# A row gradient on one core: the first store of each group of three behind most of the second tile's vector pass, that pass in two parts, and more row ends placed by Pool

## The chip, the core and the metric

The kernel runs on one core of a Trainium2 chip, launched once. The core has a vector engine (DVE in the profile), a general engine (POOL, "Pool" here), a queue engine that only issues transfers here (SP, its queue SPq), and 16 DMA engines that move data between the device memory (HBM) and the on-chip memory. A tensor engine and a scalar engine exist and do nothing in this kernel. The metric is the device time of one execution in microseconds; lower is better.

## The reference

```python
def setup_inputs():
    return {
        "x": np.random.randn(8192, 8192).astype(np.float32),
    }

def reference(x: np.ndarray) -> np.ndarray:
    return np.gradient(x, axis=1)
```

Along each row, an inner element of the result is half the difference of its right and left neighbour. The first is x[1] - x[0], the last x[8191] - x[8190], both without the half. 268.44 MB are read and as many written, with one subtraction and one scaling for each element.

## The kernel before

**Tiles.** The 8192 rows are cut into 32 tiles ("sets") of 256 rows: 128 partitions with R = 2 rows each, which lie one behind the other in a partition, W = 16384 float32 columns. There are NB = 3 buffers (`slots`) of SH + W columns with SH = 64. A load writes a tile to columns 64 to 64 + W of its buffer; the result is computed in place, shifted to columns 0 to W, and stored from there. Tile i lives in buffer i % 3.

**Work on a tile**, in the order of the program:

1. Pool takes the differences at the row ends (L70): for both rows of a partition x[1] - x[0] and x[m-1] - x[m-2], into a small tensor `ends` that keeps all tiles' values. It waits for the load.
2. The vector engine makes one pass over the tile (L76), a custom instruction that subtracts and scales by 0.5, columns 1 to W - 1. It waits for Pool's differences, since it writes over the input. At the row ends it leaves wrong values.
3. The row ends are placed over them (L87), four values in a partition, by Pool where i % 5 is 1 or 3 and i < 30, otherwise by the vector engine.
4. SP issues the store (L89), which waits for the placement.
5. After every third tile SP issues the next three loads (L60). Each waits until the store of the tile that had its buffer has landed.

**Order.** The order in each engine's queue is the order of the program (`manual_schedule`). The helper `chain` declares which earlier steps an instruction must wait for, and nothing else is waited for. All 64 transfers go through SP's one queue, in the order three loads, three stores, three loads, and so on; the last group has two tiles. A group is three tiles i with i % 3 = 0, 1, 2: "first", "second" and "third" tile, load and store below. An instruction that waits on SP holds up all that stands behind it there. The first tile's pass and placement run while the second load is transferred, the second tile's while the third load is, the third tile's while the first store is.

Of the kernel before, what the change touches and what calls it, by code (L numbers as in the profile page):

```python
# [1 line left out]

# [4 lines left out]


@with_exitstack
def kernel(  # L10
    ctx: ExitStack,
    tc: tile.TileContext,
    x: bass.AP,
    out: bass.AP,
):

    nc = tc.nc
    P = nc.NUM_PARTITIONS
    n, m = x.shape
    R = 2
    NB = 3  # L30
    SH = 64
    W = R * m
    nsets = n // (P * R)
    f32 = x.dtype

    x_sets = x.rearrange("(s p t) m -> s p (t m)", p=P, t=R)
    out_sets = out.rearrange("(s p t) m -> s p (t m)", p=P, t=R)

    pool = ctx.enter_context(tc.tile_pool(name="pool", bufs=1))
    slots = [pool.tile([P, SH + W], f32, name=f"slot{k}", tag=f"slot{k}") for k in range(NB)]  # L40
    ends = pool.tile([P, nsets, R, 2], f32, name="ends", tag="ends")
    loads, stores = [], [None] * nsets
    in_front = {}

    def chain(i, ins, *needed):

        group, engine = f"slot{i % NB}", ins.ins.engine
        keep = [o.ins for o in needed]  # L50
        if in_front.get(engine, (None,))[0] == group:
            keep.append(in_front[engine][1])
        tc.declare_no_dep(ins.ins, group=group, keep=keep, reason="implied by the needed step")
        tc.add_to_no_dep_group(group, ins.ins)
        in_front[engine] = group, ins.ins
        return ins

    def load(i):
        b = slots[i % NB]
        ins = nc.sync.dma_start(out=b[:, SH : SH + W], in_=x_sets[i])  # L60
        loads.append(chain(i, ins, *([stores[i - NB]] if i >= NB else [])))

    with tc.manual_schedule():
        for i in range(NB):
            load(i)
        for i in range(nsets):
            b = slots[i % NB]
            xin = b[:, SH : SH + W].rearrange("p (t m) -> p t m", m=m)

            ins = nc.gpsimd.tensor_sub(  # L70
                out=ends[:, i, :, :],
                in0=xin[:, :, 1 : m : m - 2],
                in1=xin[:, :, 0 : m - 1 : m - 2],
            )
            at = [chain(i, ins, loads[i])]
            ins = nc.vector._custom_dve(  # L76
                dve_ops.TENSOR_TENSOR_REDUCE_SUB_MAX,
                out=b[:, 1 : W - 1],
                in0=b[:, SH + 2 : SH + W],
                in1=b[:, SH : SH + W - 2],  # L80
                s0=0.0,
                s1=0.5,
            )
            halved = chain(i, ins, *at)
            res = b[:, 0:W].rearrange("p (t m) -> p t m", m=m)
            placer = nc.gpsimd if i % 5 in (1, 3) and i < nsets - 2 else nc.vector
            ins = placer.tensor_copy(out=res[:, :, 0 : m : m - 1], in_=ends[:, i, :, :])  # L87
            placed = chain(i, ins, halved)
            ins = nc.sync.dma_start(out=out_sets[i], in_=b[:, 0:W])  # L89
            stores[i] = chain(i, ins, placed)  # L90
            if i % NB == NB - 1:
                for k in range(i + 1, min(i + 1 + NB, nsets)):
                    load(k)


# [1 line left out]
_INS = ['x']  # L97
_OUTS = [((8192, 8192), 'float32')]


# [23 lines left out]
```

## Time and profile before

| | |
|---|---|
| time, median of 3 runs | 1247.99 us (1247.7 to 1248.6) |
| profiled execution, its own time | 1247.59 us |
| span of its instructions | 1245.7 us |
| moved | 268.44 MB read, 268.44 MB written, 431 GB/s over the span |
| vector engine busy | 554.6 us, 52 instructions |
| Pool busy | 8.8 us, 48 instructions |
| placement L87 on the vector engine | 20 times, mean 172 ns |
| placement L87 on Pool | 12 times, mean 190 ns |
| load, issue to landing, median | 58.0 us |
| store, issue to landing, min / median / max | 20.9 / 40.4 / 41.4 us |

A row of the timeline gives the start and the length in us, the engine, the line, the operation, what it writes and reads, and in brackets how long its engine had been idle and what ended that. Rows of SPq are the issues of transfers; "x3" joins three issues in a row, and the length is then the time from the first to the last. A row of the table by windows gives the window, its length, the busy time of DVE and of POOL with their instructions, the granted clock of the tensor engine (unused here), the share of the DMA engines and GB/s. A packet is put down to the window in which it starts, so in short windows the share can be over 1 or 0 although the engines work throughout. A group row of the page has the line, engine, operation, output and input shape, the number of instructions, busy us, mean ns, and the idle time ahead of them with what ended it.

### The profile page before, as it was taken

The page shows a single profiled execution, that of the slowest core. Times are in us where ns is not written, and L with a number is a line of the kernel's source. Part 1 is how long each engine was busy: PE and PEld are TensorE (multiplying, and loading weights), DVE is VectorE, ACT ScalarE, POOL GpSimd, SP SyncE. Part 2 cuts the span into 40 slices and gives each one's busy share as a digit, 9 for nine tenths or more (in the row PEclk, how much of TensorE's full clock was granted, in tenths as well). Part 3 has the DMA queues.
Part 4 walks back from the last instruction along what each step waited for, and adds up shares of the span by engine and source line. Part 5 has one row for each costly group of instructions (what it writes and reads, how often), then busy time and mean ns, then how long its engine had stood idle before and what let it go on. Part 6 is the DMA issues. An engine that isn't in the chain of part 4 may idle for free.

```text
span 1245.7 us, 237 instructions
## 1 busy us (share of the span) xinstructions
DVE 554.6 (45%) x52; POOL 8.8 (1%) x48
## 2 busy tenths in 40 slices
DVE  2850583069009702850582079009603840591083
POOL 0000000000000000000000000000000000000000
DMA  9999999999999999999999999999999999999999
GB/s 404 438 436 423 427 431 438 438 438 436 436 427 431 425 438 436 425 434 436 429 434 436 434 436 434 436 434 438 419 436 436 434 438 438 431 434 429 429 410 404
DMA packets 9217, 536.88 MB, mean 431 GB/s; under 512 B 1024, under 2 KB 1024, under 8 KB 1024
## 3 DMA queue, kind: packets, MB, share of 16 engines
q1 hardware_dynamic: 9216, 536.88, 99.8%
q14 instruction: 1, 0.01, 0.0%
HBM read 268.44 MB, written 268.44 MB: 431 GB/s over the span
## 4 chain that ended last, share of the span: by engine, by line
another core or an unknown queue 74%; DVE 18%; DMA 3%; issue 2%; POOL 1%; SPq 0%; POOLq 0%
DVE slot L76 18%; DMA slot<-in_x_dram 3%; POOL ends L70 0%; POOL slot L87 0%; SPq L60 0%; POOLq L119 0%; DVE slot L87 0%
## 5 line engine op out<-in xcount | busy, mean ns | idle before, releaser
L76 DVE CUSTOM_DVE_ANT_0 slot<-slot 128x16382 f32<-128x16382 f32 x32 | 551.2, 17224 | 668.7 <-POOL ends L70 668.7
L70 POOL TENSOR_TENSOR ends<-slot 128x4 f32<-128x4 f32 x32 | 6.3, 198 | 989.6 <-DMA slot<-in_x_dram 989.6
L87 POOL COPY slot<-ends 128x4 f32<-128x4 f32 x12 | 2.3, 190 | 207.9 <-DVE slot L76 207.9
L87 DVE COPY slot<-ends 128x4 f32<-128x4 f32 x20 | 3.4, 172 | 0.7
L108 POOL MEMSET const-bfloat16-1.0<- 128x1 bf16 x1 | 0.1, 101 | 0.0
L108 POOL MEMSET const-uint8-127<- 128x1 uint8 x1 | 0.1, 101 | 0.0
L108 POOL MEMSET const-float32-0.0<- 128x1 f32 x1 | 0.1, 98 | 0.2 <-issue 0.2
L108 POOL MEMSET const-float32-1.0<- 128x1 f32 x1 | 0.1, 98 | 0.0
## 6 DMA issues: line engine op xcount, KB each, us to landing
slot<-in_x_dram SPq DMA_DIRECT2D x32, 58.0
out_dram<-slot SPq DMA_DIRECT2D x32, 40.4
```

The costliest lines, as they stand in the source:

```text
L70: ins = nc.gpsimd.tensor_sub(out=ends[:, i, :, :], in0=xin[:, :, 1 : m : m - 2], in1=xin[:, :, 0 : m - 1 : m - 2],)
L76: ins = nc.vector._custom_dve(dve_ops.TENSOR_TENSOR_REDUCE_SUB_MAX, out=b[:, 1 : W - 1], in0=b[:, SH + 2 : SH + W], in1=b[:, SH : SH + W - 2],
L87: ins = placer.tensor_copy(out=res[:, :, 0 : m : m - 1], in_=ends[:, i, :, :])
L108: nc = _bacc.Bacc("TRN2", target_bir_lowering=False, num_devices=1)
```

## The change

Four edits.

- `opens` holds for the second tile of the ten full groups (i % 3 = 1 and i < 30). For it the vector pass goes in two instructions, columns 1 to W - 1 - 1472 and from there to W - 1. The other tiles' passes stay whole.
- The store of the first tile of a group is no longer issued in the first tile's own turn. It stands in SP's queue behind the first part of the second tile's pass in the program, and waits for that part as well as for its own placement (`store_behind`). It is still ahead of the second tile's store.
- Pool places the row ends of the first and third tile of each full group (20 tiles), the vector engine those of the second tile and of the last two tiles (12).
- The stores of the last two tiles, and all second and third stores, are issued in their own turn as before.

```diff
+    LATE = 1472
...
+    def store(i, placed):
+        ins = nc.sync.dma_start(out=out_sets[i], in_=slots[i % NB][:, 0:W])
+        stores[i] = chain(i, ins, placed)
+        return ins
+
+    def store_behind(i, placed, other):
+        tc.add_manual_dep(
+            store(i, placed).ins,
+            other.ins.name,
+            mybir.DependencyInfo(mybir.DependencyClass.Sync, mybir.DependencyReason.DATA),
+            reason="the first store of a group goes behind the second tile's difference",
+        )
...
+            opens = i % NB == 1 and i < nsets - 2
...
-            at = [chain(i, ins, loads[i])]
-            ins = nc.vector._custom_dve(
-                dve_ops.TENSOR_TENSOR_REDUCE_SUB_MAX,
-                out=b[:, 1 : W - 1],
-                in0=b[:, SH + 2 : SH + W],
-                in1=b[:, SH : SH + W - 2],
-                s0=0.0,
-                s1=0.5,
-            )
-            halved = chain(i, ins, *at)
+            halved = chain(i, ins, loads[i])
+            edges = [1, W - 1 - LATE, W - 1] if opens else [1, W - 1]
+            for c0, c1 in zip(edges, edges[1:]):
+                ins = nc.vector._custom_dve(
+                    dve_ops.TENSOR_TENSOR_REDUCE_SUB_MAX,
+                    out=b[:, c0:c1],
+                    in0=b[:, SH + c0 + 1 : SH + c1 + 1],
+                    in1=b[:, SH + c0 - 1 : SH + c1 - 1],
+                    s0=0.0,
+                    s1=0.5,
+                )
+                halved = chain(i, ins, halved)
+                if opens and c0 == 1:
+                    store_behind(i - 1, placed, halved)
             res = b[:, 0:W].rearrange("p (t m) -> p t m", m=m)
-            placer = nc.gpsimd if i % 5 in (1, 3) and i < nsets - 2 else nc.vector
+            placer = nc.gpsimd if i % NB != 1 and i < nsets - 2 else nc.vector
             ins = placer.tensor_copy(out=res[:, :, 0 : m : m - 1], in_=ends[:, i, :, :])
             placed = chain(i, ins, halved)
-            ins = nc.sync.dma_start(out=out_sets[i], in_=b[:, 0:W])
-            stores[i] = chain(i, ins, placed)
+            if i % NB or i >= nsets - 2:
+                store(i, placed)
```

More of the change, by code (lines that the diff above doesn't have):

```diff
@@ L4 @@
 import concourse.tile as tile
-from concourse import bass_utils, dve_ops
+from concourse import bass_utils, dve_ops, mybir
 from concourse._compat import with_exitstack
```

## The prediction

> **What bounds the kernel.** I read the page first: the two engines, the DMA row, the byte counts.
>
> ```profile
> DVE 554.6 (45%) x52; POOL 8.8 (1%) x48
> ...
> DMA  9999999999999999999999999999999999999999
> ...
> DMA packets 9217, 536.88 MB, mean 431 GB/s; under 512 B 1024, under 2 KB 1024, under 8 KB 1024
> ...
> q1 hardware_dynamic: 9216, 536.88, 99.8%
> ...
> L76 DVE CUSTOM_DVE_ANT_0 slot<-slot 128x16382 f32<-128x16382 f32 x32 | 551.2, 17224 | 668.7 <-POOL ends L70 668.7
> ```
>
> The DMA engines are busy in every slice and at 99.8% in sum, the vector engine at 45%, so only the rate of the transfers can change the time. There are 64 transfers (32 loads, 32 stores) of 536.88/64 = 8.39 MB. Of 9216 packets 1024 are tiny, one per engine and transfer (64 x 16); the other 8192 carry 65.5 KB each, 8 per engine and transfer.
>
> Next, the timeline gives the pace. Pool's end differences at L70 start as soon as their load has landed (idle ended by the DMA), so their starts are landing times. Four groups and the last pair, with the queue's first stores:
>
> ```profile
> 40.40 40.06 SPq L89 DMA_DIRECT2D out_dram<-slot  x3
> 42.04 0.20 POOL L70 TENSOR_TENSOR ends<-slot 128x4 f32<-128x4 f32 x1 [19.13 <-DMA slot<-in_x_dram]
> ...
> 62.44 0.20 POOL L70 TENSOR_TENSOR ends<-slot 128x4 f32<-128x4 f32 x1 [2.69 <-DMA slot<-in_x_dram]
> ...
> 157.63 39.09 SPq L89 DMA_DIRECT2D out_dram<-slot  x3
> 159.25 0.20 POOL L70 TENSOR_TENSOR ends<-slot 128x4 f32<-128x4 f32 x1 [1.65 <-DMA slot<-in_x_dram]
> ...
> 178.70 0.20 POOL L70 TENSOR_TENSOR ends<-slot 128x4 f32<-128x4 f32 x1 [19.25 <-DMA slot<-in_x_dram]
> ...
> 974.22 0.20 POOL L70 TENSOR_TENSOR ends<-slot 128x4 f32<-128x4 f32 x1 [19.15 <-DMA slot<-in_x_dram]
> ...
> 993.55 0.20 POOL L70 TENSOR_TENSOR ends<-slot 128x4 f32<-128x4 f32 x1 [19.13 <-DMA slot<-in_x_dram]
> ...
> 1186.93 0.20 POOL L70 TENSOR_TENSOR ends<-slot 128x4 f32<-128x4 f32 x1 [77.07 <-DMA slot<-in_x_dram]
> ...
> 1204.62 19.69 SPq L89 DMA_DIRECT2D out_dram<-slot  x2
> 1206.28 0.20 POOL L70 TENSOR_TENSOR ends<-slot 128x4 f32<-128x4 f32 x1 [19.14 <-DMA slot<-in_x_dram]
> ```
>
> From the first load of a group to its second, the ten full groups take 19.33, 19.36, 19.33, 19.35, 19.33, 19.35, 19.34, 19.34, 19.34 and 19.35, together 193.42, mean 19.34 us. This is the undisturbed transfer, 2.42 us a packet on each engine. From the second to the third they take 20.40, 19.45, 19.51, 20.05, 19.85, 19.79, 19.45, 19.84, 19.33 and 19.36, together 197.03: an **excess of 3.61 us**, and only in the load that has a store behind it. From the third load to the next group's first (three stores and a load) the ten stretches add to 773.77 against 40 x 19.342 = 773.68: nothing to gain there. The rest, 22.71 to the first landing, 19.35 for the last pair and 39.4 after it, has no group's first store in it. So 3.61 us, 0.29% of the time, is all that a change to that store can win by these rows.
>
> Two facts bear on why the third load is late. In the last pair the store was issued at 1204.62, 1.66 us ahead of the landing at 1206.28, and the load took 19.35: no excess. In the ten groups the first store is queued some 21 us ahead (178.70 - 157.63 = 21.07). And the windows of the DMA show how far the engines are in step (a packet counts where it starts):
>
> ```profile
> 58.00:59.00 1.00, 1.00 (x1) 0.00 (x0) 1.00 3.28 983
> 59.00:61.00 2.00, 0.50 (x1) 0.19 (x1) 1.00 0.00 0
> 61.00:62.00 1.00, 0.00 (x0) 0.00 (x0) 1.00 2.28 983
> ...
> 987.00:988.00 1.00, 1.00 (x1) 0.00 (x0) 1.00 0.76 328
> 988.00:989.00 1.00, 1.00 (x1) 0.00 (x0) 1.00 1.36 590
> ```
>
> In the first group 15 of 16 engines (983 GB/s for 1 us = 983 KB, at 65.5 KB each) begin the third load's last packet within one microsecond, start nothing for two, and begin the next packet in 61 to 62: some 3 us for a packet of 2.42. The excess is in that last packet, at the turn from load to store. In the ninth group starts are scattered over all windows, and there is no excess.
>
> **The change, part by part.**
>
> *The later store.* Today SP issues the first store when the first tile's pass and placement end. Afterwards it also waits for the first part of the second tile's pass. That part has 16382 - 1472 = 14910 columns; at 17.224 us for 16382 that is 15.68 us, the second part 1.55 us. From the second load's landing: 0.23 us to the pass (42.04 to 42.27), 15.68, and 0.03 us to the queue (the first placement ends at 40.37, the issue is at 40.40): issue at +15.94. The third load lands at +19.34, so the store is queued 3.40 us ahead instead of 21.07. Its own start-up is not exposed: a store on an idle queue takes 20.9 us at least from issue to landing, thus 20.9 - 19.34 = 1.56 us over its transfer, and 3.40 - 1.56 = 1.84 us of margin remain. Issued at 1204.62, the last pair's store started no packet before 1205.4, then all 16 by 1206.0: 0.8 us from the issue, so the new store reaches the engines about 2.6 us before the landing, when each begins its last packet of the load.
>
> What it is worth I bound from both sides. The last pair's row (lead 1.66 us) prices the excess at nothing: minus 3.61. The groups' rows (21.07) keep it whole: 0. The first group's row, in step and with 1.06 us of excess, would cost ten times 1.06 - 3.61 = plus 7.0. A lead of 3.40 stands nearest to 1.66, so I take **minus 3.61**.
>
> A rule of the Trainium skill speaks against the change: "DMA: Bandwidth & Descriptors", section "Rules for kernel authors", says to issue a DMA early, so that its fixed cost overlaps. By that rule the delay can win nothing, and the sum would be zero or worse; this trace has the early store followed by the slower load, and the late one in the last pair by none. The same page, "Anatomy of one DMA", puts the fixed cost of a transfer near 2.0 us; by it the margin would be 3.40 - 2.0 = 1.4 us, an estimate, where the row of 20.9 leaves 1.84.
>
> *What waits behind the store on SP.* Its own queue holds the second store, the third, then the three loads. The second store follows 1.9 us later (the rest of the pass 1.55, the placement 0.17, hand-offs), 18 us before the first store can have been carried out, so its place in the DMA queue is never empty. The third store and the loads keep their triggers. Cost 0; if the margin of 1.84 us were missed, every microsecond more would be an idle DMA microsecond, ten times over.
>
> *The pass in two parts.* Ten more vector instructions. The smallest vector row, the placement, has 0.172 us, the gap between two dependent ones is 0.03; so 10 x 0.2 us at most, and below nothing isn't possible as the same columns are computed. Cover: the pass ends near +17.5, its placement at +17.9, and the third load lands at +19.34, so 1.4 us of idle vector time takes it. Cost 0, without cover 2 us.
>
> *More placements on Pool.* Now 12 on Pool, afterwards the first and third tile of ten groups, 20; on the vector engine 12 instead of 20. Pool takes 0.190 against 0.172 us, and the hand-off from the pass to the issue 0.29 instead of 0.23 us (157.34 to 157.63; 40.17 to 40.40). The first tile's issue no longer hangs on it, the second tile's moves to the vector engine, and the third store waits behind two stores of 19.3 us. Pool's next end difference comes 1.6 us after the first tile's placement, or 58 us after the third's. Cost 0; without cover 20 x 0.06 = 1.2 us.
>
> **Sum.** 1247.59 (profiled execution's own time; its span is 1245.7, the other 1.9 us lie around it) - 3.61 = 1243.98. The median of the runs is 1247.99, 0.40 over that execution: **1244.4 us**, -0.29%.
>
> **Rivals.**
>
> *The store still arrives too early* (no effect). It reaches the engines while the last packets of the load are under way, and a turn that overlaps reads and writes may need nothing more. For: 2.6 us is a full packet, and in the last pair the queue was already empty (no packet start from 1204.6 to 1205.4). Against: queued 21 us ahead, the store goes with 0.45 us or more of excess in five groups of ten, queued 1.66 us ahead with 0.01, and 3.40 is nearer to the latter. Time 1248.0. Between the two, half of the excess goes: 1246.2.
>
> *Re-alignment* (slower). Engines that have run ahead drain and then all start with the store, as the sixteen did within 1205.4 to 1206.0. The 3 us by which the engines drift apart over the run seem to hide the turn: 1.06 us of excess in step, 0.01 in the ninth group. If the late store puts the engines in step ten times and does not remove the turn, each group pays up to the first one's price: 1248.0 + 7.0 = 1255.0. It decides from an average of 0.36 + 0.25 = 0.61 us of excess a group (2.5 us more in ten). For: the two windows above. Against: the second and third group, hardly apart yet, pay 0.11 and 0.17; and only engines more than about 2 us ahead would wait.
>
> **How the numbers follow.** About 0.2%, 2.5 us, is what a measurement of this kernel tells from no change. Forecast 0.50 (1244.4, own range 1243.2 to 1245.6: the runs' spread of 0.9 us and the 0.1 us of the other stretches below, 1.2 us of lost cover above); half of the excess 0.12 (1246.2); no effect 0.15 (1248.0); re-alignment 0.23 (1250.5 to 1255). Faster: the forecast and a third of the half case, 0.54. Same: the rest of these and no effect, 0.23. Slower: 0.23. The range goes from 1243.2 to 1251.0: it leaves out most of the re-alignment, some 0.19.
>
> **What would show it.** Right: the ten intervals from second to third load add to 193.4 to 194 instead of 197.03, with the first store's issue some 3.4 us ahead of the third landing, and the other stretches unchanged. No effect: still near 197. Re-alignment: all ten nearer to 20.4, and 15 or 16 packet starts within one microsecond at every turn, late groups too. I am wrong altogether if the stretch of three stores and a load grows over 77.4 us, which would mean a queue run dry or a price of the turn moved into the store.

## The result, and the profile after

The changed kernel takes 1250.12 us (median of 22 runs, 1245.17 to 1251.73) where the kernel before takes 1247.88 us in the same comparison (22 runs, 1247.16 to 1249.39). The ratio of the means is 1.0014 with a 95% interval of [1.0008, 1.0021]: slower by 0.14% (0.18% by the medians), a loss clear of noise and smaller than the 0.2% at which the prediction drew its line. The profiled execution took 1249.7 us by its own time, with a span of 1247.6 us against 1245.7.

The page of the changed kernel, its DMA and its passes:

```profile
DMA  9999999999999999999999999999999999999999
...
DMA packets 9217, 536.88 MB, mean 430 GB/s; under 512 B 1024, under 2 KB 1024, under 8 KB 1024
...
q1 hardware_dynamic: 9216, 536.88, 99.8%
...
L106 POOL COPY slot<-ends 128x4 f32<-128x4 f32 x20 | 3.8, 192 | 346.4 <-DVE slot L93 346.4
L106 DVE COPY slot<-ends 128x4 f32<-128x4 f32 x12 | 2.1, 172 | 0.4
```

The DMA engines are as busy as before. No queue ran dry; the same bytes took longer on engines that were always at work. The groups by line with shapes kept apart price the two parts of the pass:

```profile
L93 DVE CUSTOM_DVE_ANT_0 slot<-slot 128x14910 f32<-128x14910 f32 x10 | 156.9, 15691 | 21.2 <-POOL ends L85 21.2
L93 DVE CUSTOM_DVE_ANT_0 slot<-slot 128x1472 f32<-128x1472 f32 x10 | 16.9, 1693 | 0.3
```

Together 17.38 us instead of 17.22, all of it in idle time of the vector engine. The timeline of the first and of the eighth group shows the store where the change puts it:

```profile
42.11 0.20 POOL L85 TENSOR_TENSOR ends<-slot 128x4 f32<-128x4 f32 x1 [1.61 <-DMA slot<-in_x_dram]
...
58.06 21.58 SPq L65 DMA_DIRECT2D out_dram<-slot  x3
...
61.57 0.20 POOL L85 TENSOR_TENSOR ends<-slot 128x4 f32<-128x4 f32 x1 [19.26 <-DMA slot<-in_x_dram]
...
857.50 0.20 POOL L85 TENSOR_TENSOR ends<-slot 128x4 f32<-128x4 f32 x1 [1.65 <-DMA slot<-in_x_dram]
...
873.45 22.44 SPq L65 DMA_DIRECT2D out_dram<-slot  x3
...
877.82 0.20 POOL L85 TENSOR_TENSOR ends<-slot 128x4 f32<-128x4 f32 x1 [20.12 <-DMA slot<-in_x_dram]
```

The first store of the first group is issued at 58.06, 3.51 us ahead of the third landing at 61.57. There the third load takes 19.46 us instead of 20.40: the excess is nearly gone. In the eighth group it takes 877.82 - 857.50 = 20.32, more than the 19.84 of before. In both groups the store is issued 15.95 us behind the second landing, as forecast (15.94); what differs is the third landing. Over the ten groups the third loads take 19.46, 19.50, 19.51, 20.01, 19.35, 20.04, 19.75, 20.32, 19.66 and 20.40, together 198.00 against 197.03 before. The stretches of three stores and a load add to 774.26 against 773.77. With 0.97 and 0.49, and 0.07 in the second loads, 0.08 ahead of the first landing and 0.30 behind the last one, the whole difference of the spans, 1.9 us, is accounted for.

Where the eighth group's 20.32 comes from is seen in the windows around its turn from load to store. A row gives the window, its length, DVE and POOL busy, the clock, the DMA share and GB/s; GB/s times length over 65.5 KB is the number of packets that start, and share times length times 16 over that number is the mean time of one of them:

```profile
872.20:872.80 0.60, 0.60 (x1) 0.00 (x0) 1.00 3.53 1529
872.80:873.80 1.00, 0.97 (x2) 0.00 (x0) 1.00 0.00 0
873.80:874.00 0.20, 0.20 (x1) 0.00 (x0) 1.00 2.13 655
874.00:874.60 0.60, 0.60 (x1) 0.00 (x0) 1.00 0.00 0
874.60:875.20 0.60, 0.57 (x2) 0.00 (x0) 1.00 3.54 1529
875.20:877.10 1.90, 0.16 (x1) 0.00 (x0) 1.00 0.00 0
877.10:877.60 0.50, 0.00 (x0) 0.00 (x0) 1.00 4.84 2097
```

Fourteen engines begin the load's last packet within 0.6 us, need 3.53 x 0.60 x 16 / 14 = 2.42 us for it and begin the store's first one: no slow packet. **Two engines lag by 1.5 us** (873.8 to 874.0), and between 874.0 and 877.1 there are just the fourteen starts of the others: the two need 2.13 x 0.20 x 16 / 2 = 3.4 us for that packet. For the fourteen, the store, issued at 873.45, came while the packet was under way; for the two it came about when theirs began. A load has landed when the last engine is done, so the two decide.

At the turn from store to load that ended the group before, the same execution shows:

```profile
813.60:814.10 0.50, 0.00 (x0) 0.00 (x0) 1.00 5.27 1835
814.10:816.55 2.45, 0.00 (x0) 0.00 (x0) 1.00 0.12 53
816.55:817.15 0.60, 0.00 (x0) 0.00 (x0) 1.00 3.63 1529
```

Fourteen starts, then two (the laggards), then fourteen. A packet of 2.42 us begun by 814.1 would be followed by 816.52; none of the fourteen is: 5.27 x 0.50 x 16 / 14 = 3.0 us. The slow packet that the fourteen no longer have at load-to-store stands here. In the kernel before, the first group's engines are in step too and have none at this turn; sixteen packets begin, each takes 2.42 us, and sixteen follow:

```profile
116.90:117.70 0.80, 0.00 (x0) 0.00 (x0) 1.00 3.02 1311
117.70:119.30 1.60, 0.00 (x0) 0.00 (x0) 1.00 0.00 0
119.30:120.10 0.80, 0.00 (x0) 0.00 (x0) 1.00 3.04 1311
```

The changed kernel's stretch with the slow packets is no longer for them, 77.38 us, as four undisturbed transfers take 77.37. The two laggards have no slow packet there and land last; they catch up some 0.6 us of their lag at this turn, and pay at the next load-to-store.

### The profile page after: what moved, and what is told of

The parts are those of the page before. It is cut to its first block, busy times and chain, and to the rows that moved or that the text cites. A ratio compares the mean times of both kernels' runs of the same rounds, so it can differ in the third digit from the quotient of the medians.

```text
span 1247.6 us, 247 instructions
## 1 busy us (share of the span) xinstructions
DVE 554.8 (44%) x54; POOL 10.4 (1%) x56
## 3 DMA queue, kind: packets, MB, share of 16 engines
q1 hardware_dynamic: 9216, 536.88, 99.8%
## 4 chain that ended last, share of the span: by engine, by line
another core or an unknown queue 65%; DVE 28%; DMA 3%; issue 2%; POOL 1%; SPq 0%; POOLq 0%
DVE slot L93 28%; DMA slot<-in_x_dram 3%; POOL ends L85 0%; POOL slot L106 0%; SPq L61 0%; POOLq L138 0%; DVE slot L106 0%
## 5 line engine op out<-in xcount | busy, mean ns | idle before, releaser
L93 DVE CUSTOM_DVE_ANT_0 slot<-slot 128x16382 f32<-128x16382 f32 (+2 forms) x42 | 552.8, 13161 | 670.3 <-POOL ends L85 670.0
```

The costliest lines, as they stand in the source:

```text
L93: ins = nc.vector._custom_dve(dve_ops.TENSOR_TENSOR_REDUCE_SUB_MAX, out=b[:, c0:c1], in0=b[:, SH + c0 + 1 : SH + c1 + 1], in1=b[:, SH + c0 ...
```

## The experiments

The names used below: the *excess* of the third loads is their sum over 193.42 us, that of the *stretches* (three stores and a load) their sum over 773.68.

**The parts alone.** First the placements on the kernel before:

```diff
-            placer = nc.gpsimd if i % 5 in (1, 3) and i < nsets - 2 else nc.vector
+            placer = nc.gpsimd if i % NB != 1 and i < nsets - 2 else nc.vector
```

> The kernel before with the new rule of placements alone. Theory 'moved excess' (the late store only shifts the slow packet from the turn load-to-store to the turn store-to-load, and a few lagging engines still pay at the old place): no effect, 1247.2 to 1248.8 us, third loads together 196 to 198 us. Rival 'the parts cost' (placements on Pool or the split pass delay something): 0.5 to 2.5 us slower than before.

Measured: 1248.07 us beside 1248.37, ratio 0.9999 [0.999, 1.0008]; third loads 196.95. Then the pass in two parts, with store and placements as in the kernel before; the edit is against the changed kernel:

```diff
-                if opens and c0 == 1:
-                    store_behind(i - 1, placed, halved)
...
-            placer = nc.gpsimd if i % NB != 1 and i < nsets - 2 else nc.vector
+            placer = nc.gpsimd if i % 5 in (1, 3) and i < nsets - 2 else nc.vector
...
-            if i % NB or i >= nsets - 2:
-                store(i, placed)
+            store(i, placed)
```

> The kernel before with the second tile's pass in two parts alone, the store as early as before. Theory 'moved excess': no effect, 1247.2 to 1248.8 us. Rival 'the parts cost': 0.5 to 2.5 us slower.

Measured: 1248.30 beside 1248.37, ratio 0.9998 [0.9989, 1.0006]; third loads 197.00. Neither part costs or gains anything that can be told; what the change does, the wait does. The two profiles also serve as repeats of the kernel before: third loads and stretches together take 970.58 and 970.99 us, where it has 970.80.

**The wait, longer and shorter.** These edits are against the changed kernel. The store behind the whole second pass:

```diff
-            edges = [1, W - 1 - LATE, W - 1] if opens else [1, W - 1]
+            edges = [1, W - 1]
```

> The changed kernel with the second tile's pass whole again, and the first store behind all of it: the store is issued some 1.7 us later than with the two parts. Theory 'moved excess': now the lagging engines too get the store only at the end of their last load packet, so the third loads together fall to 193.4 to 194.5 us, but the turn store-to-load keeps its slow packet of 0.4 to 0.7 us in every group; time 1245 to 1248 us, faster than the changed kernel. Rival 'starved queue' (every delay of the store leaves engines idle): the stretches with three stores grow with the delay, 1252 us or more.

Measured: 1252.94 us beside 1248.37, ratio 1.0038 [1.0025, 1.005]. The third loads fall to 193.59, the excess is gone in all ten groups; the stretches rise to 782.03, 8.35 over the sum without excess. The windows of its sixth group, first three at load-to-store, last three at store-to-load:

```profile
643.00:643.60 0.60, 0.60 (x1) 0.00 (x0) 1.00 4.03 1748
643.60:645.50 1.90, 1.19 (x2) 0.00 (x0) 1.00 0.00 0
645.50:646.00 0.50, 0.00 (x0) 0.00 (x0) 1.00 4.90 2097
...
701.20:701.60 0.40, 0.00 (x0) 0.00 (x0) 1.00 7.76 2621
701.60:704.20 2.60, 0.00 (x0) 0.00 (x0) 1.00 0.00 0
704.20:704.80 0.60, 0.00 (x0) 0.00 (x0) 1.00 4.20 1748
```

All sixteen engines go from load to store in step and without a slow packet (4.03 x 0.60 x 16 / 16 = 2.4 us). All sixteen then need 7.76 x 0.40 = 3.1 us for the packet at store-to-load. This is the clearest single run: the price has **moved whole from one turn to the other**, and there it is larger. The rival 'starved queue' had named this time too, 1252 us or more with longer stretches, so the time does not decide. The windows do: at load-to-store, where a late store would leave a gap, sixteen packets follow sixteen with none, and the DMA share is 99.8% as before.

Of the expectation the two halves about the packets came true, the time did not. I had put the price of the new place at 0.4 to 0.7 us in each group; it is 2.05 in the first stretch and 0.59 to 0.90 in the other nine. The time that I expected did not even follow from my own terms: 4 to 7 us lost against 2.5 to 3.6 won is slower than the kernel before, not faster.

Then 8192 columns kept back instead of 1472:

> The changed kernel with 8192 instead of 1472 columns kept back: the first store is issued about 10 us ahead of the third load's landing, long before any engine begins its last packet of that load. Theory 'moved excess': the slow packet goes back to the turn load-to-store, third loads together 196 to 198.5 us, time 1247 to 1249 us as before. Rival 'the parts cost': stays at 1249.5 to 1251 us like the changed kernel, since split, wait and placements are all there.

Measured: 1248.72 beside 1248.37, ratio 1.0004 [0.9995, 1.0013]; third loads 198.33, stretches 773.43. The price is back at load-to-store, with split, wait and placements all in place. And 2944:

> The changed kernel with 2944 columns kept back: the store is issued 1.55 us earlier, about 4.9 us ahead of the third landing, so that it reaches most engines before they begin the last packet of the load. If the beginning of that packet is the border, the slow packet is back at load-to-store in all engines and gone from store-to-load: third loads 196 to 199 us together, time 1247.5 to 1249.5 us. If the border lies earlier, it behaves like the changed kernel, 1249.5 to 1251 us.

Measured: 1248.94 beside 1248.08, ratio 1.0007 [0.9998, 1.0016]; third loads 199.25, stretches 773.10. The sums show the price at load-to-store again and nothing at store-to-load on the engines that decide. "In all engines" did not come true: in the trace's packets five or six engines of the sixteen are slow at load-to-store in the later groups, where it is mostly one or two with 1472 columns and none with 0. The medians rise as the store gets later: 1248.7, 1248.9, 1250.1 and 1252.9 us for 8192, 2944, 1472 and 0 columns kept back. Only the last two are clear of noise; the first two can be told neither from the kernel before nor from each other.

**Is the load's early queueing to blame at the other turn?** The next group's first load held back as well, behind a second vector pass over the buffer whose store has just landed. That pass is there for its duration only; what it writes is never stored.

```diff
+                o = slots[(i - 1) % NB]
+                ins = nc.vector._custom_dve(
+                    dve_ops.TENSOR_TENSOR_REDUCE_SUB_MAX,
+                    out=o[:, 1 : W - 1],
...
+                idle = chain(i - 1, ins, stores[i - 1])
+                behind(load(i + 1), idle)
+                load(i + 2, idle)
```

> The changed kernel with the whole second pass ahead of the first store, and besides the first load of the next group held back in the same way: behind an extra vector pass over the already stored second buffer (work for timing only, its values are never stored), started when the second store has landed, so that this load too is issued some 2 us ahead of the end of the third store. Theory A (a transfer queued early in the other direction slows the last packet at its turn, and late ones are free): both turns free, about 1244 to 1246 us, three-stores stretches 77.3 to 77.5 us. Theory B (a late store takes from the engines the lead that their reading side had over their writing side, and one latency of 0.4 to 0.9 us is paid wherever reading from the device memory starts without that lead): holding the load back wins nothing, 1251 to 1255 us, three-stores stretches 78 us and more.

Measured: 1256.63 us beside 1248.08, ratio 1.007 [1.0056, 1.0084]; third loads 193.79, stretches 785.28. Theory A is out: with both transfers late, the turn is not free. Theory B has its stretches (over 78 us each), but the time is above its 1251 to 1255 us. A slow packet is now the load's own first one (the load was issued at 703.67):

```profile
703.67 2.49 SPq L61 DMA_DIRECT2D slot<-in_x_dram  x3
```

```profile
705.10:705.80 0.70, 0.00 (x0) 0.00 (x0) 1.00 4.09 1498
705.80:707.80 2.00, 0.00 (x0) 0.00 (x0) 1.00 0.00 0
707.80:708.50 0.70, 0.00 (x0) 0.00 (x0) 1.00 3.24 1404
```

Sixteen starts, 4.09 x 0.70 = 2.9 us each in the mean, and fifteen starts 2.0 to 3.4 us on. The DMA share is 99.5% here, 0.3% or some 4 us less than with the whole pass alone. That is as much as the 3.25 us by which the stretches are longer, so a dearer packet is not shown. The same hold on the kernel before, store early:

> The kernel before, store early, with only the first load of the next group held back by the extra vector pass (timing only). Theory A: no gain at load-to-store (third loads 196 to 198 us) and none to lose at store-to-load, 1247 to 1249 us. Theory B: the load starts without a lead, 0.4 to 0.9 us more in each of the ten stretches with three stores (together 777 to 782 us); the third loads may fall, as the lead that they give back is gone; 1248 to 1257 us.

Measured: 1281.2 us (4 runs, 1276.92 to 1283.02), ratio 1.0262 [1.0246, 1.0277], outside both expectations. It does not answer its question, because its queue ran dry:

```profile
q1 hardware_dynamic: 9216, 536.88, 98.2%
```

That is 1.6% less than in the kernel before, some 20 us of idle engines. The hold begins when the slowest engine has landed the second store; that engines ahead of it then wait is the likely reason. One thing it does show: drained ten times, most of the engines are in step (in most groups one lags by a packet), and its third loads take 20.07 to 20.77 us, together 204.69, 1.1 us of excess in the mean.

**Engines in step.** The kernel before with the third load held back behind the first tile's pass, which makes the engines wait for each other once a group at a turn from load to load:

```diff
+            if i % NB == 0 and 0 < i and i + 2 < nsets:
+                behind(load(i + 2), halved)
```

> The kernel before, store early, with the third load of each later group held back until the first tile's pass is over, some 2 us ahead of the second load's landing: it makes engines that ran ahead wait once a group, at a turn from load to load, and leaves the turn load-to-store as it was. My rival of the prediction (engines in step pay 1.06 us at load-to-store): third loads near 20.4 us in all groups, together 202 to 205 us, time 1253 to 1257 us. Against it: third loads together 196 to 199 us, 1247 to 1250 us.

Measured: 1271.49 us beside 1248.08, ratio 1.0188 [1.0172, 1.0204]; third loads 220.99, stretches 773.98. The windows of its sixth group at the third load's first packet (above) and last packet (below):

```profile
634.50:635.40 0.90, 0.00 (x0) 0.00 (x0) 1.00 3.38 1165
635.40:637.60 2.20, 1.88 (x1) 0.20 (x1) 1.00 0.00 0
637.60:638.10 0.50, 0.50 (x1) 0.00 (x0) 1.00 4.84 2097
652.10:652.50 0.40, 0.40 (x1) 0.00 (x0) 1.00 8.98 2621
652.50:655.60 3.10, 0.44 (x1) 0.19 (x1) 1.00 0.00 0
655.60:656.30 0.70, 0.00 (x0) 0.00 (x0) 1.00 3.47 1498
```

The held-back load's first packet takes 3.38 x 0.90 = 3.0 us although a load went before it, as after a store in the run with both transfers held. Then, with the store queued early, the last packet at load-to-store takes 8.98 x 0.40 = 3.6 us. In the first group of the kernel before, also in step, the same working with the row in the prediction gives 3.28 x 16 / 15 = 3.5 us, so the rival's price for engines in step is confirmed in this group's packets. The time is outside both expectations and does not price it: the intervals are 21.14 to 24.21 us from the second group on and hold both prices and the waiting, and the DMA share falls to 99.1%.

**Which groups.** The late store in the first group alone, and in all but the first:

```diff
+            late = opens and i < 3
...
-                if opens and c0 == 1:
+                if late and c0 == 1:
```

> The changed kernel with the late store in the first group alone; the other nine first stores as early as before. By the profiled intervals the first group (second to third load and the stretch behind it) took 97.85 us before and 96.99 us in the changed kernel, the others gained nothing. Theory 'by group' (only where all engines are in step and none lags does the late store win): 0.86 us faster than the kernel before, some 1247.2 to 1247.6 us beside 1248.1. Rival 'any late store costs' (the price of the sweep, 2 us for ten groups, is spread evenly): 0.2 us slower than before.

Measured: 1247.62 beside 1247.81, ratio 0.9999 [0.999, 1.0008]. The time decides nothing: 0.86 us faster and 0.2 us slower both lie in the interval. In the profile the first group's third load takes 19.34, 1.06 less than before; but the second group's takes 20.62, where it takes 19.45, 19.63 and 19.48 in the three profiles with every first store early. All third loads add to 197.04, as before. In this profile the engines that were spared the first turn paid at the next one with an early store.

> The changed kernel with the late store in the nine later groups alone, the first group's store as early as before. Theory 'by group': the loss of the changed kernel and 0.86 us more, 1250.5 to 1251.5 us. Rival 'any late store costs': nine tenths of the loss, about 1249.9 us.

Measured: 1251.53 beside 1247.81, ratio 1.0028 [1.0018, 1.0038]; third loads 199.20, stretches 775.26. That is just over the range of 'by group' and 1.6 us over the rival's 1249.9: the loss is the later groups' own.

**The changed kernel again.** Two more profiles:

> The changed kernel once more, for a second profile. If the lagging engines are what makes it slow, its third loads again add to 197 to 199 us with the excess in the later groups while most of the engines begin the store together without a slow packet, and the stretches with three stores to 773.5 to 775 us. If an execution near 1245 us is met, its third loads must add to some 194 to 195 us.

> As the run before it, a third profile of the changed kernel, under the same expectation.

Measured: 1250.3 and 1250.17 us; third loads 198.44 and 197.21, stretches 774.59 and 775.10 (the latter just over the range). The two sums trade with each other, their total does not: 973.03 and 972.31, and 972.26 in the first profile, against 970.58 to 970.99 in the three profiles with every first store early. No execution near 1245 us was met. Two of the 22 runs took 1245.2 and 1245.3, less than any run of the kernel before and about what was forecast; no such execution was profiled, and why it happens is open.

The total of the two sums, over 967.10 us without any excess, follows the time of the profiled execution over the places of the store, but for two pairs of close neighbours. Medians come from different comparisons, in which the kernel before took 1247.81 to 1248.37:

| kernel | third loads | stretches | both over 967.10 | profiled us | median us |
|---|---|---|---|---|---|
| late in the first group only | 197.04 | 773.39 | 3.33 | 1248.09 | 1247.62 |
| before | 197.03 | 773.77 | 3.70 | 1247.59 | 1247.88 |
| 8192 kept back | 198.33 | 773.43 | 4.66 | 1249.02 | 1248.72 |
| changed, 1472 | 198.00 | 774.26 | 5.16 | 1249.70 | 1250.12 |
| 2944 kept back | 199.25 | 773.10 | 5.25 | 1249.51 | 1248.94 |
| changed, later groups only | 199.20 | 775.26 | 7.36 | 1252.04 | 1251.53 |
| whole pass, 0 | 193.59 | 782.03 | 8.52 | 1252.63 | 1252.94 |
| and the load held back | 193.79 | 785.28 | 11.97 | 1256.59 | 1256.63 |

The traces' packets show the same move. What they take beyond 2.42 us, added over the ten groups and sixteen engines, is some 50 us at load-to-store and 3 at store-to-load before, 14 and 61 in the changed kernel, and 3 and 122 with the whole pass. No version was faster than the kernel before by more than the noise.

## Why the prediction was wrong, point by point

**What bounds the kernel** was right, and so was the place of the excess: the last packet of the third load, at load-to-store, larger with the engines in step. By the share in its own row, that packet took 3.5 us in the first group, not "some 3".

**The step that failed is what the later store is worth.** It took minus 3.61 us by the last pair's row, as the nearest in lead. Measured: plus 0.97 in the third loads and plus 0.49 in the stretches; by the two repeats plus 0.2 to 1.4 and plus 0.8 to 1.3. Two things were wrong in it. First, the last pair was no fair likeness. No load follows its stores, so a price that only moves to the next store-to-load turn cannot show there. Also, the queue there was dry when the store came: in the 2.4 us up to 1205.4, about the time of one packet, a single packet begins, and then sixteen within 0.6 us:

```profile
1203.00:1204.60 1.60, 1.56 (x2) 0.00 (x0) 1.00 0.10 41
1204.60:1205.40 0.80, 0.00 (x0) 0.00 (x0) 1.00 0.00 0
1205.40:1206.00 0.60, 0.00 (x0) 0.00 (x0) 1.00 4.08 1748
```

The run with the whole pass had the lead of that row (644.65 to 646.51, 1.86 us) in all groups, removed the excess as the row says, and paid 8.35 us in the stretches. Second, "so the new store reaches the engines about 2.6 us before the landing, when each begins its last packet of the load" treated sixteen engines as one. The landing that it reckons from is the slowest engine's. The store comes when the fourteen are in the middle of their last packet, and they are spared; the two laggards begin theirs about then, are not spared, and decide the landing. So the changed kernel pays in both places.

**"Nothing to gain there"** of the stretches was read rightly from the rows and taken wrongly as "nothing to lose". The prediction's last sentence named 77.4 us as the mark beyond which a price has moved into the store, or a queue run dry; the mean is now 77.43, hardly over it, and 78.20 in the whole-pass run.

**The margin** was right: issue 3.4 to 4.4 us ahead, no idle engines (99.8%), not even at 1.86 us. The 2.0 us that the prediction cites beside it stand in the page under the path through the general engine; here all transfers go through SP, and the row of 20.9 us is what counts. **SP's order** was right. **The split** was right: a part of 1472 columns takes 1.69 instead of the 1.55 us estimated, covered, and the run with the split alone shows no cost. **The placements** were right, likewise.

**The rivals.** "No effect" and half of the excess are out by the interval. Re-alignment was half right: the late store does put engines in step, and engines in step do pay (1.1 us and more at an early-queued turn when forced), but with a late store the price falls due at the next turn. The measured 2.2 us is below the 2.5 from which that rival was to count. The 1250.12 us lie inside the stated range, up to 1251.0, only because the range had been drawn to take in a part of this rival; the sum itself pointed the other way.

That a later store moves the price from load-to-store to store-to-load is shown, by the two sums and the packets at both turns with 8192, 1472 and 0 columns kept back. It is no fixed amount: with the whole pass it is more than twice what it was. How an engine holds it is argued only. In the Trainium skill, the page "DMA: Bandwidth & Descriptors" says in its section "Two DMAs through the same engine are not ordered" that the descriptors of one queue start in order on an engine but are pipelined, and that an engine's reading and writing sides are separate queues. A reading side that keeps a lead over the writing side, loses it when a transfer arrives late, and then exposes a latency at the next load would fit; no run here shows the two sides apart.

## What to carry to other kernels

Where the DMA engines are always busy, an excess at one turn of direction is not yet a gain: find the next turn of the same cycle and see what it costs once the first is cured, and take as a likeness only a row that has such a next turn. A transfer's time is its slowest engine's, so a trigger tuned to a fraction of a packet hits some engines early and some late. Of the positions tried here none was faster than queueing the store as early as possible, and the two latest were slower, though the queue did not run dry.

## What the runs showed of the hardware

- A packet of 65.5 KB takes 2.42 us on one engine, and 3.0 to 3.6 us in the slow rows shown at a turn of direction. With most engines in step and the store queued early, the third loads took 1.1 us more each (20.07 to 20.77 us in the run whose queue drained); in the ninth group of the kernel before, where the engines were scattered, there was no excess (19.33).
- A load held back until the last moment had a first packet of 2.9 to 3.0 us in the windows shown, after a load as well as after a store.
- Two of sixteen engines, 1.5 us behind, decided the time of whole transfers (20.32 us in the eighth group).
- In one profile, sparing the first group's turn its price (1.06 us) went with a dearer turn in the next group, by 1.17 us (20.62 against 19.45).
